# Seven block products in place of eight in the gate stage of a two-group decoder layer on eight cores

## The chip, the cores and the metric

One Trainium2 chip, all 8 cores. The metric is the device time of the slowest core, in microseconds. Two programs share the chip. Even cores ("half 0") take the first 976 positions of a prompt and a quarter of the sampling group, 1216 output columns each. Odd cores ("half 1") take the rest of the prompt, 1088 output columns, and recompute part of the first half for its state. Some executions fall in a slow state, in which one die, sometimes both, gets a lower clock. Unless said otherwise only fast runs are compared.

## The reference

One layer: a gated mixer of two branches, then a squared-ReLU feed-forward. The change touches the merge of the branches:

```python
xa, ga, q, k, v, g, gate_a, gate_b = split_proj(h @ w_in)      # h: rmsnorm(x), D_MODEL = 2048
...                                                            # ya: RG-LRU branch, yb: retention branch
merged = jax.nn.sigmoid(gate_a) * (ya @ p_a) + jax.nn.sigmoid(gate_b) * (yb @ p_b)
return merged @ w_out, new_buf, h_last, S_last
```

## The kernel before

Operations are recorded in program order with the memory they touch. A list scheduler then places each where it can start earliest by its own estimates of durations; every engine executes that order strictly. So an estimate decides the order of instructions, and a buffer decides what may be placed where. The estimate for VectorE ("dve"):

```python
elif meth == "tensor_tensor" and all(isinstance(x, bass.AP) and x.dtype in TWO for k, x in kw.items() if k != "op"):
    dur = 150 + 0.53 * n          # two-input operation, everything 16 bits wide, n elements per partition
```

The gate stage, behind the eight retention heads. `wA` and `wB` are block m of the two gates (16 x 128 x 128 each), `wp` the two branch projections:

```python
nE = min(6, (rt.e - rt.p) // al(4 * OW))
tb = [M.f32(rt(4 * OW), OW) for _ in range(nE)]
r1 = Reg(R1, A_R[2])
tb += [M.f32(r1(4 * OW), OW) for _ in range(16)]             # 22 temporaries
...
for m in range(16):
    wA, wB = wfm(40 + m), wfm(56 + m)
    wp = wload(T["w_p"][m], 2, 8, 128)
    for a, b in cf.och:                                       # three chunks of 362 or 364 columns (odd cores)
        n = b - a
        ts_ = []
        gops = []
        for w in (wA, wB):                                    # 2 x 16 matmuls
            pt = PT()
            gops.append(group(pt, w, hT, a + lead, b + lead))
            t = tnew()
            P.v("dve", "tensor_tensor", out=t[:, 0:n], in0=pt(0, n), in1=rbc[:, a + lead:b + lead], op=ALU.mult)
            P.v("act", "activation", out=t[:, 0:n], in_=t[:, 0:n], func=AF.Sigmoid)
            ts_.append(t)
        for z, y in enumerate((yaT, ybT)):                    # 2 x 8 matmuls
            ...
        P.v("pool", "tensor_tensor", out=mT[:, m, a:b], in0=ts_[0][:, 0:n], in1=ts_[1][:, 0:n], op=ALU.add)
```

The feed-forward's up and down stages (not shown) already compute each 2x2 arrangement of blocks with seven products and sums of weights and activations, the Strassen-Winograd scheme, in passes of 272 columns on odd cores.

Of the kernel before, what the change touches and what calls it, by code (L numbers as in the profile page):

```python
# [12 lines left out]
ALU = mybir.AluOpType  # L13
# [130 lines left out]
class Prog:  # L144
# [86 lines left out]
    def v(self, eng, meth, after=(), **kw):  # L231
        reads, writes, pr, pw = [], [], [], []
        n_ap = 0
        psum = False
        for k, x in kw.items():
            if isinstance(x, PV):
                (pw if k in ("out", "accum_out") else pr).append(x.pt)
                psum = True
            elif isinstance(x, bass.AP):
                (writes if k in ("out", "accum_out") else reads).append(x)  # L240
                if k in ("scale", "bias") or k.startswith("scalar"):
                    n_ap += 1
        n = self._n(kw["out"])
        tabs = None
        if meth == "bn_stats":
            dur = 280
        elif meth == "bn_aggr":
            dur = 175
        elif eng == "act":
            dur = (170 if psum else 225) + 0.833 * n + 45 * n_ap  # L250
            if meth == "activation":
                tabs = TABS.get(kw["func"])
        elif eng == "dve":
            if meth == "tensor_tensor_scan":
                dur = 90 + 2.5 * n
            elif meth == "reciprocal":
                dur = 60 + 6.5 * n
            elif meth in ("tensor_scalar", "tensor_copy", "tensor_scalar_mul") and not psum:
                dur = 190 + 0.66 * n
            elif meth == "tensor_tensor" and all(isinstance(x, bass.AP) and x.dtype in TWO for k, x in kw.items() if k != "op"):  # L260
                dur = 150 + 0.53 * n
            else:
                dur = (160 if psum else 220) + 1.05 * n + (100 if psum and n_ap > 1 else 0)
        elif meth == "tensor_tensor":
            dur = 260 + 1.92 * n
        elif meth == "tensor_copy":
            dur = 250 + 1.12 * n
        else:
            dur = 260 + 2.4 * n
        banks = self.banks  # L270

        def fn(e):
            a = {k: (x.ap(banks) if isinstance(x, PV) else x) for k, x in kw.items()}
            return getattr(e, meth)(**a)  # L274
        return self._new(eng, fn, reads, writes, pr, pw, dur, tabs, after=after)
# [375 lines left out]
    return v.rearrange("p (s t) -> p s t", t=3)  # L651

NSLOT = 7
HS = 16.0
US = 64.0
C0 = C_OFF["mask"][0]
# [9 lines left out]
A_VW = 0  # L666
# [4 lines left out]
def record(nc, P, M, T, cf):  # L671
# [19 lines left out]
            return a  # L691

    r3 = Reg(R3, A_CST)
    hT = M.bf(o_h, 16, NT)
    yaT = M.bf(o_ya, 8, NO)
    ybT = M.bf(o_yb, 8, NO)
    x1T = M.f32(0, 16, NO)
    Q = NO // 4
    RS, TS = 64 * Q, 48 * Q
# [6 lines left out]
    L_TMP = L_ACC + 4 * NO  # L706
    NTT = min(4, (A_KC - L_TMP) // (4 * Q))
    assert NTT >= 3
    mT = M.bf(A_R[2], 16, NO)
    assert A_R[2] + 32 * NO <= A_SLOT + 8192  # L710
    CW = max(b - a for a, b in cf.ch)
    OW = max(b - a for a, b in cf.och)
# [7 lines left out]
    def wload(src, *shape, at=None, after=()):  # L720
        if at is None:
            at = slots[wctr[0] % nring[0]]
            wctr[0] += 1
        w = M.bf(at, *shape)
        wf = w.rearrange("p a b -> p (a b)") if len(shape) == 2 else w.rearrange("p a b c -> p (a b c)")
        w_last[0] = P.dma("pool", wf, src, after=after)
        return w
# [253 lines left out]
    if cf.npre:  # L981
        NP = cf.npre
        NPT = len(cf.ptiles)
        hTq = M.bf(R2, 16, NP)
        rbcp = M.f32(R2 + 32 * NP, NP)
        assert R2 + 36 * NP <= R3
        r1 = Reg(R1, R2)
        Ls = [lru_set(r1, NP, 0, False) for _ in range(2)]
        vw, kw = M.bf(A_VW, 16, 512), M.bf(A_VW + 16384, 16, 512)
        nmax = 384  # L990
        vpp = M.bf(rt(1024 * NPT), NPT, 4, 128)
        kpp = [M.bf(rt(1024), 512) for _ in range(2)]
# [117 lines left out]
    o_cos = rt(4 * NT)  # L1110
    cosT = M.f32(o_cos, NT)
    sinT = M.f32(rt(4 * NT), NT)
    vq = [M.bf(r2(4096), 4, 512) for _ in range(2)] + [M.bf(o_yb + 4096 * i, 4, 512) for i in range(2)]
    assert o_yb + 8192 <= o_vh0

    def v_load(hg):
# [226 lines left out]
    for h in range(8):  # L1343
        if h < 7:
            proj(h + 1)
        attn(h)

    rt = Reg(TMPE, TEND)
    nE = min(6, (rt.e - rt.p) // al(4 * OW))
    tb = [M.f32(rt(4 * OW), OW) for _ in range(nE)]  # L1350
    r1 = Reg(R1, A_R[2])
    tb += [M.f32(r1(4 * OW), OW) for _ in range(16)]
    tc = [0]

    def tnew():
        x = tb[tc[0]]
        tc[0] += 1
        if tc[0] == len(tb):
            tc[0] = nE
        return x  # L1360

    del slots[0:2]
    nring[0] = len(slots)
    for m in range(16):
        wA, wB = wfm(40 + m), wfm(56 + m)
        wp = wload(T["w_p"][m], 2, 8, 128)
        for a, b in cf.och:
            n = b - a
            ts_ = []
            gops = []  # L1370
            for w in (wA, wB):
                pt = PT()
                gops.append(group(pt, w, hT, a + lead, b + lead))
# [1 line left out]
                P.v("dve", "tensor_tensor", out=t[:, 0:n], in0=pt(0, n), in1=rbc[:, a + lead:b + lead], op=ALU.mult)  # L1375
                P.v("act", "activation", out=t[:, 0:n], in_=t[:, 0:n], func=AF.Sigmoid)
                ts_.append(t)
            for z, y in enumerate((yaT, ybT)):
                pt = PT()
                P.mm([(pt(0, n), wp[:, z, k, :], y[:, k, a:b], k == 0, k == 7, "m") for k in range(8)], after=gops)  # L1380
                P.v("dve", "tensor_tensor", out=ts_[z][:, 0:n], in0=pt(0, n), in1=ts_[z][:, 0:n], op=ALU.mult)
            P.v("pool", "tensor_tensor", out=mT[:, m, a:b], in0=ts_[0][:, 0:n], in1=ts_[1][:, 0:n], op=ALU.add)


    accv = M.f32(L_ACC, NO)
# [9 lines left out]
    def sum_sq(m, x, a, b, e="pool"):  # L1395
        if m == 0:
            P.v("act", "activation", out=accv[:, a:b], in_=x, func=AF.Square)
        else:
            sq = sqs[m % 2]
            P.v("act", "activation", out=sq[:, 0:b - a], in_=x, func=AF.Square)  # L1400
            P.v(e, "tensor_tensor", out=accv[:, a:b], in0=accv[:, a:b], in1=sq[:, 0:b - a], op=ALU.add)

    def t_sums(src, t1, t2, t4, e=("dve",) * 4):

        b11, b12, b21, b22 = src
        P.v(e[0], "tensor_tensor", out=t1, in0=b12, in1=b11, op=ALU.subtract)
        P.v(e[1], "tensor_tensor", out=t2, in0=b22, in1=t1, op=ALU.subtract)
        P.v(e[2], "tensor_tensor", out=t4, in0=b21, in1=t2, op=ALU.subtract)
        P.v(e[3], "tensor_tensor", out=b12, in0=b22, in1=b12, op=ALU.subtract)

    spill = []
    wslots = [L_SLOT + 4096 * i for i in range(2, 6)]
# [1 line left out]
    for m in range(16):  # L1414
# [16 lines left out]
            spill.append(P.dma("sp", T["x1"][(m - 12) * 128 * NO:(m - 11) * 128 * NO].rearrange("(p n) -> p n", p=128), xt))  # L1431
        if m >= 8:
            i = m - 8
            t_sums([raw2[:, :, 4 * i + q, :] for q in range(4)], *[tq2[:, :, 8 * k + i, :] for k in range(3)])

    def rs_rows(a, b):
        pt = PT()
# [7 lines left out]
    def wset(src):  # L1445
# [4 lines left out]
        wb = M.hf(L_SLOT + 4096 * (2 * n % 6 + 1), 2, 1024)  # L1450
        for w, x in ((wa, src[0]), (wb, src[1])):
            P.dma("pool", w.rearrange("p a b -> p (a b)"), x)
        s1, s2, s4 = (M.hf(L_S + 2048 * ((3 * n + i) % 6), 1024) for i in range(3))
        a11, a12, a21, a22 = wa[:, 0, :], wa[:, 1, :], wb[:, 0, :], wb[:, 1, :]
        P.v("dve", "tensor_tensor", out=s1, in0=a21, in1=a22, op=ALU.add)
        P.v("dve", "tensor_tensor", out=s2, in0=s1, in1=a11, op=ALU.subtract)
        P.v("dve", "tensor_tensor", out=s4, in0=a12, in1=s2, op=ALU.subtract)
        P.v("dve", "tensor_tensor", out=a21, in0=a11, in1=a21, op=ALU.subtract)
        v = lambda x: x.rearrange("p (k c) -> p k c", k=8)
        return [v(x) for x in (a11, a12, s4, a22, s1, s2, a21)]  # L1460

    def prod(pt, w, x, first):
        P.mm([(pt(0, Q), w[:, k, :], x[:, k, :], first and k == 0, k == 7, "m" if first else "g") for k in range(8)])

    tmp = [M.f32(L_TMP + 4 * Q * i, Q) for i in range(NTT)]
    tmp_d = tmp + [M.f32(L_ACC + 4 * Q * i, Q) for i in range(4)]
# [94 lines left out]
    def u_sums(b, s, h):  # L1561
        j = 2 * b + 2 + s
        k = slice(4 * h, 4 * h + 4)
        r = rawq[j % 3][:, k]
        t = tq[j % 2][:, :, k]
        t_sums([r[:, :, q] for q in range(4)], *[t[:, i] for i in range(3)])

    def order(n, head):
        o = [(0, 0), (1, 0), (0, 1), (1, 1)] if head else [(0, 0), (0, 1), (1, 0), (1, 1)]
# [348 lines left out]
```

## Time and profile before

| | before |
|---|---|
| median of all 15 runs, this comparison | 2045.35 us |
| span, odd cores / even cores | 2036 to 2039 / 2024 to 2028 us |
| PE busy, slowest core | 95% |
| gate stage, odd cores | about 328 us |

The lines of the profile that carry this stand in the prediction. How to read them: PE is TensorE, DVE is VectorE, ACT is ScalarE and POOL is GpSimd; a bank is a piece of PSUM, the memory into which PE writes, and an evacuation is another engine's operation that reads a bank. "Busy" of a matmul is modelled, so durations come from periods; a bracket `[0.50 <-ACT arena L274]` says that the engine stood idle for 0.50 us until ACT finished; nearly all operations have the line of a recording helper (L274, L305, L307), so shapes tell them apart.

### The profile page before, as it was taken

How to read it: one execution, taken by the hardware profiler on the slowest of the kernel's cores; microseconds unless marked ns; L12 is line 12 of the kernel's file. 1: busy time of each engine (PE TensorE's matmuls, PEld its weight loads, DVE VectorE, ACT ScalarE, POOL GpSimd, SP SyncE). 2: the span in 40 equal slices, each digit the busy share in tenths (PEclk: the TensorE clock that was granted, in tenths of full speed). 3: DMA queues.
4: the chain of work that ended last, by engine and by line, in shares of the span. 5: the costliest groups of instructions: out<-in, count | busy, mean ns of one | idle time of the engine just before them, and what ended most of it. 6: DMA issues, size and time to landing. Idle time of an engine off the chain costs nothing.

```text
span 2039.2 us, 40316 instructions; the slowest of 8 cores (2024.5 to 2039.2 us)
## 1 busy us (share of the span) xinstructions
PE 1935.6 (95%) x14400; PEld 1384.5 (68%) x14400; DVE 1032.3 (51%) x1898; ACT 734.8 (36%) x1573; POOL 932.1 (46%) x1212
## 2 busy tenths in 40 slices
PE   4788799998999999999999999999999999999997
PEld 2444455555666666666678888888888778888567
DVE  3577634663334332222234565555556667675245
ACT  4455525675554411111123454444444111111123
POOL 5654752335666421211124454444444556555544
PEclk9998999999999999999999999999999999999998
DMA  8844732332332343443437766666667756565822
GB/s 224 145 104 117 160 74 42 54 61 43 66 65 45 55 83 63 82 74 63 73 84 147 177 126 157 135 123 126 127 126 163 175 108 137 86 159 85 187 78 99
DMA packets 83214, 219.20 MB, mean 107 GB/s; under 512 B 10176, under 2 KB 34496, under 8 KB 81216
## 3 DMA queue, kind: packets, MB, share of 16 engines
q0 software_dynamic: 38448, 139.05, 40.7%
q1 hardware_dynamic: 40816, 73.04, 11.0%
q10 hardware_dynamic: 3744, 4.46, 0.6%
q8 instruction: 118, 1.93, 0.4%
q14 instruction: 88, 0.72, 0.1%
HBM read 326.04 MB, written 29.51 MB: 174 GB/s over the span
## 4 chain that ended last, share of the span: by engine, by line
PE 83%; DVE 5%; issue 4%; DMA 4%; POOL 2%; ACT 2%; POOLq 0%; DVEq 0%; ACTq 0%; SPq 0%
PE bank L305 68%; PE bank L307 15%; DVE arena L274 5%; POOL arena L274 2%; DMA arena<-xo 2%; DMA arena<-w_tm 1%; ACT arena L274 1%; PE bank L303 0%; DMA arena<-w_dn 0%; POOL arena L321 0%; ACT L274 0%; DVEq L601 0%; POOLq L1726 0%; POOLq L601 0%; ACTq L601 0%
## 5 line engine op out<-in xcount | busy, mean ns | idle before, releaser
L305 PE MATMUL bank<-arena 128*128 128x272 f16 (+14 forms) x11408 | 1631.9, 302 | 69.9 <-DVE arena L274 50.0
L305 PEld LDWEIGHTS bank<-arena 128*128 128x128 bf16 (+3 forms) x11408 | 1098.8, 99 | 554.7 <-issue 97.5
L274 POOL TENSOR_TENSOR arena<-arena 128x272 f32<-128x272 f32 (+17 forms) x830 | 720.7, 880 | 651.8 <-DVE arena L274 402.5
L274 ACT ACTIVATE arena<-arena 128x272 f32<-128x272 f32 (+15 forms) x940 | 464.4, 518 | 797.8 <-DVE arena L274 608.3
L274 DVE TENSOR_TENSOR arena<-bank,arena 128x272 f32<-128x272 f32 (+8 forms) x794 | 391.0, 496 | 677.9 <-PE bank L305 478.9
L307 PE MATMUL bank<-arena 128*128 128x272 f16 (+3 forms) x2848 | 372.5, 278 | 21.1 <-POOL arena L274 9.5
L307 PEld LDWEIGHTS bank<-arena 128*128 128x128 f16 (+3 forms) x2848 | 277.6, 99 | 82.8 <-issue 28.8
L274 DVE TENSOR_TENSOR arena<-arena 128x1024 f16<-128x1024 f16 (+7 forms) x335 | 274.9, 832 | 33.3 <-ACT arena L274 13.1
L274 DVE SCALAR_TENSOR_TENSOR arena<-bank,arena 128x272 f32<-128x272 f32 (+6 forms) x392 | 170.8, 446 | 190.5 <-PE bank L305 118.2
L274 ACT ACTIVATE arena<-bank 128x272 f32<-128x272 f32 (+8 forms) x128 | 47.3, 374 | 304.9 <-PE bank L307 165.2
L274 DVE SCALAR_TENSOR_TENSOR arena<-arena 128x976 f32<-128x976 f32 (+5 forms) x110 | 125.3, 1169 | 33.3 <-ACT arena L274 32.4
L274 ACT COPY arena<-bank 64x384 f32<-64x384 f32 (+5 forms) x216 | 89.8, 424 | 78.6 <-DVE arena L274 30.9
L321 POOL DMA_DIRECT2D arena<-w_fm x80 | 45.5, 570 | 152.7 <-PE bank L305 133.8
L274 ACT ACTIVATE arena<-bank,arena 128x128 bf16<-128x128 f32 (+2 forms) x168 | 72.6, 513 | 34.4 <-PE bank L305 18.1
L321 POOL DMA_DIRECT2D arena<-w_up x64 | 37.6, 588 | 97.9 <-PE bank L307 87.6
L274 DVE TENSOR_SCALAR arena<-arena 128x384 bf16<-128x384 f32 (+5 forms) x104 | 57.0, 576 | 44.0 <-DMA arena<-xo 26.4
L274 ACT ACT_TABLE_LOAD x49 | 62.9, 1283 | 37.5 <-DVE arena L274 19.1
L321 POOL DMA_DIRECT2D arena<-w_dn x64 | 36.1, 566 | 61.7 <-DVE arena L274 37.9
L274 DVE TENSOR_TENSOR_SCAN arena<-arena 128x976 f32<-128x976 f32 (+1 forms) x16 | 38.5, 2406 | 6.4 <-POOL arena L274 6.4
L274 POOL COPY arena<-arena 128x3 f32<-128x3 f32 (+1 forms) x40 | 16.5, 413 | 53.1 <-DVE arena L274 46.2
L274 ACT CAST arena<-bank 128x128 bf16<-128x128 f32 x72 | 19.1, 266 | 42.6 <-PE bank L307 42.0
L274 POOL TENSOR_SCALAR arena<-arena 128x256 bf16<-128x256 f32 (+6 forms) x36 | 27.8, 788 | 12.1 <-DMA arena<-xp 7.2
(17 smaller groups left out, 110.2 us busy)
## 6 DMA issues: line engine op xcount, KB each, us to landing
arena<-w_fm POOLq DMA_DIRECT2D x80, 512.0 KB, 6.4
arena<-w_up POOLq DMA_DIRECT2D x64, 512.0 KB, 6.1
arena<-w_dn POOLq DMA_DIRECT2D x64, 512.0 KB, 6.9
u_hold<-arena SPq DMA_DIRECT2D x48, 272.0 KB, 3.7
arena<-u_hold SPq DMA_DIRECT2D x12, 1088.0 KB, 8.9
arena<-w_tm POOLq DMA_DIRECT2D x24, 512.0 KB, 10.4
arena<-xr SPq DMA_DIRECT2D x64, 136.0 KB, 3.6
arena<-w_o POOLq DMA_DIRECT2D x16, 512.0 KB, 6.4
```

Source lines behind the costliest of these rows:

```text
L274: return getattr(e, meth)(**a)
L305: r = e.matmul(out.ap(banks), lhsT=lhsT, rhs=rhs, start=start, stop=stop)
L307: r = e.matmul(out.ap(banks), lhsT=lhsT, rhs=rhs, start=start, stop=stop, skip_group_check=True)
L321: return e.dma_start(out=out, in_=in_)
```

## The change

Intent: gate blocks m = 2 to 15 with seven products instead of eight. The two gate blocks are the row halves of a 2x2 matrix, the two halves of the contraction its columns, and the tokens are split in two. Blocks 0 and 1 stay plain, to keep PE busy while VectorE forms the activation sums. Activations and weights become 16-bit floats with the longer fraction (`hf`), because sums of them are rounded too. The scheduler's estimate for 16-bit two-input operations rises. The core of the diff, cut where marked:

```diff
-                dur = 150 + 0.53 * n
+                dur = 291 + 0.529 * n
...
+GSTD = 2
...
-    hT = M.bf(o_h, 16, NT)
-    yaT = M.bf(o_ya, 8, NO)
-    ybT = M.bf(o_yb, 8, NO)
+    hT = M.hf(o_h, 16, NT)
+    yaT = M.hf(o_ya, 8, NO)
+    ybT = M.hf(o_yb, 8, NO)
...                                    (mT, the weight slots and the projections' weights likewise)
-    tb += [M.f32(r1(4 * OW), OW) for _ in range(16)]
...
+    tb = [M.f32(rt(4 * OW), OW) for _ in range(min(6, (rt.e - rt.p) // al(4 * OW)))]
...
-    for m in range(16):
-        wA, wB = wfm(40 + m), wfm(56 + m)
-        wp = wload(T["w_p"][m], 2, 8, 128)
+    for m in range(GSTD):
+        wA, wB, wp = gate_loads(m)
...                                    (the plain loop, as before)
+    H2 = NO // 2
+    hq = [hT[:, 8 * k:8 * k + 8, lead + H2 * n:lead + H2 * n + H2] for k in range(2) for n in range(2)]
+    TB = al(16 * H2)
+    th = [M.hf(a, 8, H2) for a in (R2, R2 + TB, R1 + TB, R1)]
+    for k in range(8):
+        t_sums([x[:, k, :] for x in hq], *[t[:, k, :] for t in th])
...
+    for m in range(GSTD, 16):
+        wA, wB, wp = gate_loads(m)
+        w = w_sums(*[x.rearrange("p (h k) c -> p h (k c)", h=2) for x in (wA, wB)], *[sring[(3 * m + i) % 6] for i in range(3)])
+        for s in range(2):
...
+            prod(X, a11, b11, True)
+            P.v("act", "copy", out=u2, in_=X(0, Q))
+            prod(Y, s2, t2, True)
+            P.v("dve", "tensor_tensor", out=u2, in0=Y(0, Q), in1=u2, op=ALU.add)
+            prod(Z, s1, t1, True)
+            P.v("dve", "tensor_tensor", out=y4, in0=Z(0, Q), in1=u2, op=ALU.add)
+            prod(W, s3, t3, True)
+            P.v("dve", "tensor_tensor", out=y4, in0=W(0, Q), in1=y4, op=ALU.add)
+            gate_out(y4, r2)
+            prod(X, a12, b21, False)
+            P.v("dve", "tensor_tensor", out=y1, in0=X(0, Q), in1=r1, op=ALU.mult)
+            gate_out(y1, None)
+            prod(Z, s4, b22, False)
+            P.v("dve", "tensor_tensor", out=y2, in0=Z(0, Q), in1=u2, op=ALU.add)
+            gate_out(y2, r2)
+            e = prod(W, a22, t4, False)
+            P.v("dve", "tensor_tensor", out=u2, in0=W(0, Q), in1=u2, op=ALU.add)
+            gate_out(u2, r1)
...                                    (four branch projections of 8 matmuls, the merge on pool)
```

More of the change, by code (lines that the diff above doesn't have):

```diff
@@ L708, in record @@
     assert NTT >= 3
-    mT = M.bf(A_R[2], 16, NO)
+    mT = M.hf(A_R[2], 16, NO)
     assert A_R[2] + 32 * NO <= A_SLOT + 8192
@@ L723, in wload @@
             wctr[0] += 1
-        w = M.bf(at, *shape)
+        w = M.hf(at, *shape)
         wf = w.rearrange("p a b -> p (a b)") if len(shape) == 2 else w.rearrange("p a b c -> p (a b c)")
@@ L983, in record @@
         NPT = len(cf.ptiles)
-        hTq = M.bf(R2, 16, NP)
+        hTq = M.hf(R2, 16, NP)
         rbcp = M.f32(R2 + 32 * NP, NP)
@@ L988, in record @@
         Ls = [lru_set(r1, NP, 0, False) for _ in range(2)]
-        vw, kw = M.bf(A_VW, 16, 512), M.bf(A_VW + 16384, 16, 512)
+        vw, kw = M.hf(A_VW, 16, 512), M.hf(A_VW + 16384, 16, 512)
         nmax = 384
@@ L1112, in record @@
     sinT = M.f32(rt(4 * NT), NT)
-    vq = [M.bf(r2(4096), 4, 512) for _ in range(2)] + [M.bf(o_yb + 4096 * i, 4, 512) for i in range(2)]
+    vq = [M.hf(r2(4096), 4, 512) for _ in range(2)] + [M.hf(o_yb + 4096 * i, 4, 512) for i in range(2)]
     assert o_yb + 8192 <= o_vh0
@@ L1346, in record, with t_sums, w_sums, prod @@
         attn(h)
+    def t_sums(src, t1, t2, t3, t4):
+        b11, b12, b21, b22 = src
+        P.v("dve", "tensor_tensor", out=t1, in0=b12, in1=b11, op=ALU.subtract)
+        P.v("dve", "tensor_tensor", out=t2, in0=b22, in1=t1, op=ALU.subtract)
+        P.v("dve", "tensor_tensor", out=t4, in0=b21, in1=t2, op=ALU.subtract)
+        P.v("dve", "tensor_tensor", out=t3, in0=b22, in1=b12, op=ALU.subtract)
+    def w_sums(wa, wb, s1, s2, s4):
+        a11, a12, a21, a22 = wa[:, 0, :], wa[:, 1, :], wb[:, 0, :], wb[:, 1, :]
+        P.v("dve", "tensor_tensor", out=s1, in0=a21, in1=a22, op=ALU.add)
+        P.v("dve", "tensor_tensor", out=s2, in0=s1, in1=a11, op=ALU.subtract)
+        P.v("dve", "tensor_tensor", out=s4, in0=a12, in1=s2, op=ALU.subtract)
+        P.v("dve", "tensor_tensor", out=a21, in0=a11, in1=a21, op=ALU.subtract)
+        v = lambda x: x.rearrange("p (k c) -> p k c", k=8)
+        return [v(x) for x in (a11, a12, s4, a22, s1, s2, a21)]
+    def prod(pt, w, x, first):
+        return P.mm([(pt(0, Q), w[:, k, :], x[:, k, :], first and k == 0, k == 7, "m" if first else "g") for k in range(8)])
+    del slots[0:2]
+    nring[0] = len(slots)
     rt = Reg(TMPE, TEND)
-    nE = min(6, (rt.e - rt.p) // al(4 * OW))
-    tb = [M.f32(rt(4 * OW), OW) for _ in range(nE)]
-    r1 = Reg(R1, A_R[2])
-    tb += [M.f32(r1(4 * OW), OW) for _ in range(16)]
+    tb = [M.f32(rt(4 * OW), OW) for _ in range(min(6, (rt.e - rt.p) // al(4 * OW)))]
     tc = [0]
     def tnew():
-        x = tb[tc[0]]
         tc[0] += 1
-        if tc[0] == len(tb):
-            tc[0] = nE
-        return x
-    del slots[0:2]
-    nring[0] = len(slots)
-    for m in range(16):
-        wA, wB = wfm(40 + m), wfm(56 + m)
-        wp = wload(T["w_p"][m], 2, 8, 128)
+        return tb[tc[0] % len(tb)]
+    def gate_loads(m):
+        return wfm(40 + m), wfm(56 + m), wload(T["w_p"][m], 2, 8, 128)
+    def p_group(wp, z, a, b, after):
+        pt = PT()
+        y = (yaT, ybT)[z]
+        P.mm([(pt(0, b - a), wp[:, z, k, :], y[:, k, a:b], k == 0, k == 7, "m") for k in range(8)], after=after)
+        return pt(0, b - a)
+    for m in range(GSTD):
+        wA, wB, wp = gate_loads(m)
         for a, b in cf.och:
             n = b - a
-            ts_ = []
-            gops = []
+            ts_, gops = [], []
             for w in (wA, wB):
@@ L1377, in record @@
                 ts_.append(t)
-            for z, y in enumerate((yaT, ybT)):
-                pt = PT()
-                P.mm([(pt(0, n), wp[:, z, k, :], y[:, k, a:b], k == 0, k == 7, "m") for k in range(8)], after=gops)
-                P.v("dve", "tensor_tensor", out=ts_[z][:, 0:n], in0=pt(0, n), in1=ts_[z][:, 0:n], op=ALU.mult)
+            for z in range(2):
+                P.v("dve", "tensor_tensor", out=ts_[z][:, 0:n], in0=p_group(wp, z, a, b, gops), in1=ts_[z][:, 0:n], op=ALU.mult)
             P.v("pool", "tensor_tensor", out=mT[:, m, a:b], in0=ts_[0][:, 0:n], in1=ts_[1][:, 0:n], op=ALU.add)
+    H2 = NO // 2
@@ new lines, in record @@
+    hq = [hT[:, 8 * k:8 * k + 8, lead + H2 * n:lead + H2 * n + H2] for k in range(2) for n in range(2)]
[3 more added lines that the diff above has]
+        t_sums([x[:, k, :] for x in hq], *[t[:, k, :] for t in th])
+    ra_, rb_ = Reg(R1 + 2 * TB, R2), Reg(R2 + 2 * TB, A_R[2])
+    sring = [M.hf(ra_(2048), 1024) for _ in range(6)]
+    tb = [M.f32(r(4 * Q), Q) for r in (rb_, ra_) for _ in range((r.e - r.p) // al(4 * Q))]
+    tc[0] = -1
@@ new lines, in gate_out @@
+    def gate_out(t, r):
+        if r is not None:
+            P.v("pool", "tensor_tensor", out=t, in0=t, in1=r, op=ALU.mult)
+        P.v("act", "activation", out=t, in_=t, func=AF.Sigmoid)
+    for m in range(GSTD, 16):
+        wA, wB, wp = gate_loads(m)
+        w = w_sums(*[x.rearrange("p (h k) c -> p h (k c)", h=2) for x in (wA, wB)], *[sring[(3 * m + i) % 6] for i in range(3)])
+        for s in range(2):
+            n1, n2 = Q * s, H2 + Q * s
+            b11, b21, b22 = (hT[:, 8 * k:8 * k + 8, lead + n:lead + n + Q] for k, n in ((0, n1), (1, n1), (1, n2)))
+            t1, t2, t3, t4 = (t[:, :, n1:n1 + Q] for t in th)
+            r1, r2 = rbc[:, lead + n1:lead + n1 + Q], rbc[:, lead + n2:lead + n2 + Q]
+            X, Y, Z, W = PT(), PT(), PT(), PT()
+            u2, y4, y1, y2 = (tnew() for _ in range(4))
+            a11, a12, s4, a22, s1, s2, s3 = w
+            prod(X, a11, b11, True)
[16 more added lines that the diff above has]
+            gate_out(u2, r1)
+            for t, z, n in ((y1, 0, n1), (y4, 1, n2), (y2, 0, n2), (u2, 1, n1)):
+                P.v("dve", "tensor_tensor", out=t, in0=p_group(wp, z, n, n + Q, [e]), in1=t, op=ALU.mult)
+            P.v("pool", "tensor_tensor", out=mT[:, m, n1:n1 + Q], in0=y1, in1=u2, op=ALU.add)
+            P.v("pool", "tensor_tensor", out=mT[:, m, n2:n2 + Q], in0=y2, in1=y4, op=ALU.add)
@@ L1401, in sum_sq @@
             P.v(e, "tensor_tensor", out=accv[:, a:b], in0=accv[:, a:b], in1=sq[:, 0:b - a], op=ALU.add)
-    def t_sums(src, t1, t2, t4, e=("dve",) * 4):
-        b11, b12, b21, b22 = src
-        P.v(e[0], "tensor_tensor", out=t1, in0=b12, in1=b11, op=ALU.subtract)
-        P.v(e[1], "tensor_tensor", out=t2, in0=b22, in1=t1, op=ALU.subtract)
-        P.v(e[2], "tensor_tensor", out=t4, in0=b21, in1=t2, op=ALU.subtract)
-        P.v(e[3], "tensor_tensor", out=b12, in0=b22, in1=b12, op=ALU.subtract)
     spill = []
@@ L1433, in record @@
             i = m - 8
-            t_sums([raw2[:, :, 4 * i + q, :] for q in range(4)], *[tq2[:, :, 8 * k + i, :] for k in range(3)])
+            v = [raw2[:, :, 4 * i + q, :] for q in range(4)]
+            t1, t2, t4 = (tq2[:, :, 8 * k + i, :] for k in range(3))
+            t_sums(v, t1, t2, v[1], t4)
     def rs_rows(a, b):
@@ L1452, in wset @@
             P.dma("pool", w.rearrange("p a b -> p (a b)"), x)
-        s1, s2, s4 = (M.hf(L_S + 2048 * ((3 * n + i) % 6), 1024) for i in range(3))
-        a11, a12, a21, a22 = wa[:, 0, :], wa[:, 1, :], wb[:, 0, :], wb[:, 1, :]
-        P.v("dve", "tensor_tensor", out=s1, in0=a21, in1=a22, op=ALU.add)
-        P.v("dve", "tensor_tensor", out=s2, in0=s1, in1=a11, op=ALU.subtract)
-        P.v("dve", "tensor_tensor", out=s4, in0=a12, in1=s2, op=ALU.subtract)
-        P.v("dve", "tensor_tensor", out=a21, in0=a11, in1=a21, op=ALU.subtract)
-        v = lambda x: x.rearrange("p (k c) -> p k c", k=8)
-        return [v(x) for x in (a11, a12, s4, a22, s1, s2, a21)]
-    def prod(pt, w, x, first):
-        P.mm([(pt(0, Q), w[:, k, :], x[:, k, :], first and k == 0, k == 7, "m" if first else "g") for k in range(8)])
+        return w_sums(wa, wb, *[M.hf(L_S + 2048 * ((3 * n + i) % 6), 1024) for i in range(3)])
     tmp = [M.f32(L_TMP + 4 * Q * i, Q) for i in range(NTT)]
@@ L1565, in u_sums @@
         t = tq[j % 2][:, :, k]
-        t_sums([r[:, :, q] for q in range(4)], *[t[:, i] for i in range(3)])
+        v = [r[:, :, q] for q in range(4)]
+        t_sums(v, t[:, 0], t[:, 1], v[1], t[:, 2])
     def order(n, head):
```

## The prediction

> **What bounds the kernel now.** I read the cores first, then the engine line of the page, then busy times by stage, then PE's waits, and last the timeline where two stages meet. Unless said otherwise a reading is of core 7, the slowest.
>
> ```profile
> core 6: 2027.6 us, clock 0.990
> core 7: 2039.2 us, clock 0.987
> ```
>
> Odd cores (1088 own columns, 2036 to 2039 us) set the end; even cores (1216 own columns) finish some 12 us earlier. All clocks are near full, so this is the fast state, and the change has to be counted for the odd cores.
>
> ```profile
> PE 1935.6 (95%) x14400; PEld 1384.5 (68%) x14400; DVE 1032.3 (51%) x1898; ACT 734.8 (36%) x1573; POOL 932.1 (46%) x1212
> ```
>
> PE is the candidate, but a mean over stages can hide another bound. The table of stretches gives start:end, length, busy us (and instructions) of PE, PEld, DVE, ACT and POOL, granted clock, DMA share, GB/s:
>
> ```profile
> 780.00:840.00 60.00, 60.00 (x393) 38.18 (x391) 17.38 (x33) 8.10 (x16) 11.44 (x15) 1.00 0.37 64
> 1300.00:1400.00 100.00, 100.00 (x866) 84.46 (x865) 57.36 (x124) 45.79 (x123) 45.08 (x61) 1.00 0.63 127
> ```
>
> The first is the gate stage (about 717 to 1041 us), the second the up-projection, which already uses seven products in place of eight. PE is full in both at clock 1.00 and nothing else is near full. So PE columns removed from the gate stage come off the end one for one, unless something new stops PE.
>
> Busy time of a matmul is modelled, so for its cost I take periods. Two evacuations of the same place in neighbouring token chunks of the gate stage:
>
> ```profile
> 1021.71 0.54 DVE L274 TENSOR_TENSOR arena<-bank,arena 128x362 f32<-128x362 f32 x1 [1.92 <-PE bank L305]
> ...
> 1029.07 0.53 DVE L274 TENSOR_TENSOR arena<-bank,arena 128x362 f32<-128x362 f32 x1 [1.92 <-PE bank L305]
> ```
>
> A chunk is 48 matmuls: 7.36 us / 48 = 153.3 ns at 362 columns. At 272 columns the chain that ended last gives start, duration, what and count:
>
> ```profile
> 1231.62 2.78 PE bank L307 x24
> ...
> 1244.59 2.78 PE bank L307 x24
> ```
>
> These are the same point of two neighbouring passes, two column halves apart, 112 matmuls: 12.97 us / 112 = 115.8 ns.
>
> **What the Trainium skill says.** "TensorE: Matmul & The Clock Gate", section "Wait — 56ns, not 53.3ns?": start to start is columns / 2.4 GHz plus about 2.5 ns. That gives 153.3 and 115.8 ns: the trace agrees, so more but shorter matmuls pay a small fixed fee each. The peak-current note in "Seeing it yourself" speaks of 13/16 of the clock once three cores of a die run dense matmuls; the profiled run shows 0.987 to 0.993 on all eight, so I do not use it. "VectorE: DVE Perf Modes", section "The perf-mode tier table", says a two-input 16-bit operation reaches two elements per cycle, and "SBUF — State Buffer", section "SBUF: two separate sides", says that VectorE with two SBUF inputs and GpSimd take one port pair by turns, the loser waiting for the whole instruction. The trace agrees with both; the same operation twice, free and behind three POOL instructions:
>
> ```profile
> 1660.02 0.68 DVE L274 TENSOR_TENSOR arena<-arena 128x1024 f16<-128x1024 f16 x1
> ...
> 1661.53 2.19 POOL L274 TENSOR_TENSOR arena<-arena 128x272 f32<-128x272 f32 x3
> 1661.78 2.50 DVE L274 TENSOR_TENSOR arena<-arena 128x1024 f16<-128x1024 f16 x1
> ```
>
> **The change part by part.** (1) *Fewer products.* Blocks m = 2 to 15 of the gates now treat two gate blocks by two halves of the contraction by two halves of the tokens as a 2x2 product with seven block products. Columns of the gates per m: before 2 x 16 x 1088 = 34816, after 7 x 8 x 1088/2 = 30464. The branch projections keep 16 x 1088. In instructions: before 144 matmuls x 153.3 ns (7.36 x 3 chunks, 22.1 us), after 2 x 7 x 8 + 4 x 16 = 176 x 115.8 ns = 20.4 us. Saved per m: 4352/2.4 ns less 32 x 2.5 ns = 1.73 us; times 14: 24.3 us. On even cores, 4864 columns per m, 27.3 us; they stay the faster ones.
>
> (2) *Sums of activations*, once: 32 operations of 128x544 in 16 bits, at 0.44 us free and 580 ns in the mean of today's rows: 14 to 19 us of VectorE. They need neither PE nor a bank. In the order of the changed program's instructions all 32 stand ahead of the second product that needs them: eight before the attention stage, most between its last evacuations. PE has 168 further matmuls of 362 or 364 columns (25.8 us) behind the attention's last transposes. So: hidden, 0 us.
>
> (3) *Sums of weights*, per m: 4 operations of 128x1024, 712 ns each in the up stage (841 over all): 3 us. VectorE's evacuations go from 12 x 0.54 = 6.4 us to 20 x 0.44 = 8.8 us. Total some 12 of 20.4 us. POOL, per m: 10 x 0.82 us plus three DMA issues of 0.57 = 9.9 us; ACT 10 x 0.42 = 4.2 us. All below PE, at about the shares of the up stage (57, 45, 46 of 100), where PE never stops. But VectorE must not be late: behind W's first product PE has just one product (0.93 us) before it accumulates into that bank again, and an evacuation of 0.44 us with two handovers fits only if VectorE is free. A weight sum held by POOL as above would break it now and then. I take 2 us in all for 28 passes, an estimate.
>
> (4) *Weights*: the same three loads per m, cast to another 16-bit type. Landing takes 6.4 us; gate loads of the next m find their slots free one m ahead. 0 us. The rows of 128x272 f16 and 128x272 bf16 both read 279 ns, so the type costs PE nothing.
>
> (5) *Fewer spare buffers at the seam.* Today the first gate blocks fill PE's holes at the end of the attention:
>
> ```profile
> 708.41 7.89 PE L305 MATMUL bank<-arena 64*64 64x128 bf16 x50
> 716.13 0.52 PE L303 MATMUL bank<-arena 128*128 128x128 bf16 x5
> 716.58 43.65 PE L305 MATMUL bank<-arena 128*128 128x362 bf16 x283
> ```
>
> The merged row of 50 is 2 of the attention and 48 of the gates, over the normalisation's latency. The gate temporaries were 22 and can now be only six until m = 2; each chunk holds two until the last head is done. In the order of instructions, 192 gate matmuls stood before those transposes; now there are 120 and one product of eight. Missing: 72 x 153.3 - 8 x 115.8 = 10.1 us of filling. Not all of it is lost, as many fillers were longer than the hole (16 matmuls, 2.5 us, where an unfilled handover to ACT reads 0.50 us). In the last hole 4.6 us of work (24 x 153.3 + 8 x 115.8) now stand over about 7.4 us: 2.8 us idle. Add one or two unfilled handovers: 3 us lost.
>
> (6) *The scheduler's estimate* for 16-bit sums rises (for 1024 elements from 693 to 833 ns), which reorders the feed-forward too. PE waits 8.3 us for VectorE there in 13 waits; I expect between 3 us won and 3 us lost, 0 in the middle.
>
> Sum: -24.3 + 2 + 3 + 0 = -19.3 us, from a median of 2045.75: about 2026 us, 1.0% less.
>
> **The rivals.** *A, VectorE or the port lock becomes the bound in the gates.* For it: the 2.50 us row, and two more POOL additions per pass than the up stage has. Against it: the up stage with the same sums has no PE wait, and a gate pass is 88 matmuls (10.2 us) against 56. If each pass lost 0.7 us, 20 us would go and the time would stay at 2045. *B, the seam costs the whole 10 us*, or the sums placed between the attention's evacuations delay its serial state updates: 2033 us. For it, PE follows ACT there one step at a time; against it, the lost filler is partly overlong. *C, nothing is lost and the better estimate helps:* -24.3 - 3, 2018 us. *D, 16-bit floats with a longer fraction draw more current and a lower clock:* some per cent slower; against it, the feed-forward runs f16 at clock 1.00. *E, the even cores become the slowest:* no, they gain more.
>
> **Range and chances.** C and B bound the likely cases, with room at both ends: 2018 to 2034. Faster by over 2% would need under 2005, 41 us, more than all columns removed: 1%. Slower by over 2% would need D or a stall of 65 us: 1%. Within 2%: 98%.
>
> **What would show it.** Step 1: in the gate stage, from one block to the next, 20.4 us in place of 22.1, with 14 x 144 = 2016 fewer matmuls of 362 and 364 columns and 14 x 176 = 2464 more of 272. Step 3: PE's waits for VectorE in the gate stage, some 2 us; 10 or more means A. Step 5: PE idle of 3 us between the last head's projections and the last transposes; near 10 means B. Step 6: PE's waits in the feed-forward, 8.3 us today. Step 2: no PE wait for VectorE at the first products of m = 2. I am wrong in kind if PE is no longer full in the gates, or if the clocks fall.

## The result, and the profile after

The changed kernel took 2020.35 us (median of 7 runs) beside 2045.35 us of the kernel before (15 runs). The ratio of the fast runs is 0.9879, with a 95% interval of 0.9867 to 0.9891: 1.2% less, inside the 2%. A ratio here is the mean time of one kernel's fast runs over that of the other's in the same rounds, so not quite the ratio of the medians. The outputs are correct.

Spans and clocks of the changed kernel, core 7 again, and core 1, which was slowest this time:

```profile
core 1: 2020.5 us, clock 0.982
...
core 7: 2015.7 us, clock 0.985
```

The gate stage, the same table of stretches as in the prediction, core 7:

```profile
740.00:1020.00 280.00, 279.81 (x2416) 234.35 (x2414) 152.27 (x328) 56.46 (x135) 125.02 (x175) 1.00 0.44 75
```

PE is still full (279.8 of 280 us), at clock 1.00; VectorE went from 29 to 54 of 100, ACT stays low and POOL is at 45. One block of the new gates, on PE's timeline of core 7: the same place in two neighbouring blocks.

```profile
883.23 1.09 PE L307 MATMUL bank<-arena 128*128 128x272 f16 x8
...
903.61 1.09 PE L307 MATMUL bank<-arena 128*128 128x272 f16 x8
```

That is 20.38 us a block.

So where did 23 to 25 us come from? I cut the run at eight instructions that exist in both kernels: VectorE's last scan of the RG-LRU, the first and the twelfth normalised retention output (the multiplication of 128x512 from PSUM), PE's last transposes of the attention, the first scaled residual of the output projection, the first and last store of the up stage, the last load of the down stage, and the end. All are start times from the timelines, so each stretch holds waits and work together. Core 7, with differences taken before rounding (the other odd cores agree to some 1.6 us in each stretch behind the first):

| stretch, us | before | after | difference |
|---|---|---|---|
| start to last scan | 475.3 | 477.6 | +2.3 |
| to first retention output ("attention start") | 38.6 | 41.8 | +3.1 |
| to twelfth ("heads") | 151.0 | 150.3 | -0.7 |
| to last transposes ("seam") | 51.2 | 43.3 | -7.8 |
| to output projection ("gate") | 327.6 | 313.9 | -13.8 |
| output projection | 140.9 | 140.8 | -0.1 |
| up stage | 400.2 | 400.6 | +0.4 |
| down stage | 301.6 | 294.3 | -7.3 |
| last load to end | 152.8 | 153.2 | +0.5 |

Seam and gate belong together, for 10.1 us of gate matmuls only moved from in front of the last transposes to behind them. The two ends of the gate stretch, first before, then after: PE's last transposes and the first scaled residual.

```profile
716.13 0.52 PE L303 MATMUL bank<-arena 128*128 128x128 bf16 x5
1043.78 0.36 DVE L274 TENSOR_SCALAR arena<-arena 128x272 f16<-128x272 f32 x1
```

```profile
712.97 0.52 PE L303 MATMUL bank<-arena 128*128 128x128 bf16 x5
1026.82 0.36 DVE L274 TENSOR_SCALAR arena<-arena 128x272 f16<-128x272 f32 x1
```

Heads, seam and gate make 529.8 us before and 507.5 after on core 7: -22.3 (odd cores in the mean: 529.7 and 507.8). The first row has the same instruction order in both kernels on every engine. It varies from core to core, from 474 to 475 us before and from 476 to 481 us after, and the granted clock of this stretch goes with it: core 1 had 0.96 and 475.3 us before, 0.95 and 481.1 us after; over all the runs below, odd cores at 0.97 took 474 to 476 us and one at 0.93 took 484.8 us. So I don't count it as an effect of the change. That leaves three things to settle: +3.1 at the attention's start (+3.2 in the mean of the odd cores), -7.3 in the down stage, and how the -22.3 divides.

*The attention's start.* VectorE, core 7, before: scan, then evacuations of the first head's projections:

```profile
479.41 0.56 DVE L274 TENSOR_TENSOR arena<-bank,arena 128x384 f32<-128x384 f32 x1 [0.51 <-POOL arena L274]
484.60 0.56 DVE L274 TENSOR_TENSOR arena<-bank,arena 128x384 f32<-128x384 f32 x1 [4.63 <-POOL arena L274]
```

and after:

```profile
481.67 0.56 DVE L274 TENSOR_TENSOR arena<-bank,arena 128x384 f32<-128x384 f32 x1 [0.52 <-POOL arena L274]
482.14 7.64 DVE L274 TENSOR_TENSOR arena<-arena 128x544 f16<-128x544 f16 x8
489.70 0.94 DVE L274 TENSOR_TENSOR arena<-bank,arena 128x384 f32<-128x384 f32 x2
```

The scheduler put eight activation sums into a hole of 4.63 us. Free, they would take 8 x 0.44 = 3.5 us; they took 7.64 us, while POOL was working on five wide operations (below). The single records fit the lock that the prediction names: the first five sums took 1.98 and four times 1.23 us, one to each POOL operation, and the last three, with POOL done, 0.43 us each.

```profile
481.58 6.84 POOL L274 TENSOR_TENSOR arena<-arena 128x1088 f16<-128x1088 f32 x5
```

The next evacuation follows its predecessor by 8.0 us in place of 5.2. PE pays behind it: 0.8 us more in a wait for POOL (3.5 against 2.7 us), and 2.1 us more at the first state update; before, then after:

```profile
486.97 0.26 PE L307 MATMUL bank<-arena 128*128 128x128 bf16 x1 [1.06 <-ACT arena L274]
```

```profile
492.06 0.26 PE L307 MATMUL bank<-arena 128*128 128x128 bf16 x1 [3.11 <-ACT arena L274]
```

*The down stage.* PE's waits from 1160 to 1900 us (waiting engine, engine waited for, us, times, longest), before and then after:

```profile
PE bank L307 <- DVE arena L274: 6.1, 8, 1.9
PE bank L305 <- DVE arena L274: 2.2, 5, 0.8
PE bank L305 <- POOL arena L274: 1.0, 1, 1.0
```

```profile
PE bank L307 <- DVE arena L274: 1.3, 2, 1.0
PE bank L307 <- ACT arena L274: 0.2, 1, 0.2
```

7.0 us less waiting for VectorE, and the down stage is 7.3 us shorter. The change doesn't touch this stage except through the estimate and a helper's argument order.

*The seam.* The last hole of the attention, after (core 7):

```profile
707.99 5.14 PE L305 MATMUL bank<-arena 64*64 64x128 bf16 x34
712.97 0.52 PE L303 MATMUL bank<-arena 128*128 128x128 bf16 x5
713.42 2.79 PE L305 MATMUL bank<-arena 128*128 128x272 f16 x19
```

There is no wait in it, although 2.8 us of idle time had been forecast there: the last transposes come 5 us after the group of matmuls in front of the hole, where they had come 7.7 us after it with more filler. The filler had stretched the hole, not only filled it. The runs below agree: with 34, 42 and 50 matmuls in this row, of which two belong to the attention, the transposes come 5.0, 6.5 and 7.7 us after its start, without a wait (42 in runs 4, 7 and 12).

### The profile page after: what moved, and what is told of

Same layout as the page of the kernel before. It is cut to its first block, busy times and chain, and to the rows that moved or that the text cites. A ratio compares the mean times of both kernels' runs of the same rounds, so it can differ in the third digit from the quotient of the medians.

```text
span 2020.5 us, 41951 instructions; the slowest of 8 cores (1993.4 to 2020.5 us)
## 1 busy us (share of the span) xinstructions
PE 1918.5 (95%) x14848; PEld 1429.3 (71%) x14848; DVE 1127.8 (56%) x2098; ACT 753.7 (37%) x1629; POOL 1000.9 (50%) x1310
## 4 chain that ended last, share of the span: by engine, by line
PE 86%; DMA 4%; issue 3%; DVE 3%; POOL 2%; ACT 1%; SPq 0%; POOLq 0%; DVEq 0%; ACTq 0%
PE bank L305 65%; PE bank L307 20%; DVE arena L274 3%; POOL arena L274 2%; DMA arena<-xo 2%; DMA arena<-w_tm 1%; ACT arena L274 1%; DMA arena<-rtp 1%; DMA arena<-w_up 1%; PE bank L303 0%; POOL arena L321 0%; SPq L321 0%; ACT L274 0%; POOLq L1783 0%; DVEq L601 0%
## 5 line engine op out<-in xcount | busy, mean ns | idle before, releaser
L305 PE MATMUL bank<-arena 128*128 128x272 f16 (+11 forms) x11184 | 1548.2, 296 | 69.4 <-DVE arena L274 54.3
L305 PEld LDWEIGHTS bank<-arena 128*128 128x128 f16 (+2 forms) x11184 | 1079.7, 99 | 477.8 <-issue 102.3
L274 POOL TENSOR_TENSOR arena<-arena 128x272 f32<-128x272 f32 (+15 forms) x928 | 787.9, 859 | 621.1 <-DVE arena L274 366.0
L274 ACT ACTIVATE arena<-arena 128x272 f32<-128x272 f32 (+14 forms) x968 | 472.5, 509 | 743.5 <-DVE arena L274 464.5
L274 DVE TENSOR_TENSOR arena<-bank,arena 128x272 f32<-128x272 f32 (+7 forms) x906 | 423.4, 471 | 576.0 <-PE bank L305 361.7
L307 PE MATMUL bank<-arena 128*128 128x272 f16 (+1 forms) x3520 | 461.6, 278 | 19.7 <-POOL arena L274 9.6
L307 PEld LDWEIGHTS bank<-arena 128*128 128x128 f16 (+1 forms) x3520 | 341.4, 99 | 95.9 <-issue 27.9
L274 DVE TENSOR_TENSOR arena<-arena 128x1024 f16<-128x1024 f16 (+7 forms) x423 | 347.9, 833 | 30.8 <-ACT arena L274 17.2
L274 ACT COPY arena<-bank 128x272 f32<-128x272 f32 (+5 forms) x244 | 100.7, 420 | 101.1 <-PE bank L305 42.3
L274 DVE TENSOR_SCALAR arena<-arena 128x384 f16<-128x384 f32 (+5 forms) x104 | 56.4, 570 | 45.2 <-DMA arena<-xo 26.9
L274 POOL COPY arena<-arena 128x3 f32<-128x3 f32 (+1 forms) x40 | 16.2, 404 | 49.5 <-DVE arena L274 44.1
```

What stands on the lines that cost most here:

```text
L274: return getattr(e, meth)(**a)
L305: r = e.matmul(out.ap(banks), lhsT=lhsT, rhs=rhs, start=start, stop=stop)
L307: r = e.matmul(out.ap(banks), lhsT=lhsT, rhs=rhs, start=start, stop=stop, skip_group_check=True)
```

## The experiments

The theory after the result: (1) fewer products give 24.3 us; (2) eight sums at the attention's start cost 3.2; (3) the seam costs some 2; (4) the scheduler's estimate gives some 7 in the feed-forward. Rivals: the feed-forward gains through some other effect of the change, or the products give less and the rest more; the 3.2 us are chance. There were twelve runs, of nine variants and the changed kernel itself, all correct, each with 5 rounds against the kernel before. Stretches are means over the odd cores unless a core is named.

**1. The estimate alone**, in the kernel before.

```diff
-                dur = 150 + 0.53 * n
+                dur = 291 + 0.529 * n
```

> The kernel before with nothing changed but the scheduler's estimate for 16-bit two-input sums (0.291 us + 0.529 ns per element in place of 0.150 us + 0.53 ns). Theory 1 (the feed-forward gained some 7 us from the better estimate alone, as the stretch from the last store of the up stage to the last load of the down stage shrank from 301.5 to 294.3 us on core 7): the same stretch reads 294 to 295 us, the waits of PE for VectorE in the feed-forward fall from 8.3 us to under 2 us, and the time falls by 6 to 8 us (ratio 0.9965). Rival (the gain comes from the gate stage handing over differently, or from the chip of that run): the stretch stays at 301 us and the ratio is 1.000.

Ratio 0.9961 (0.9947 to 0.9975). The down stage reads 293.4 to 294.0 us; the stretches from the attention's start to the up stage stay within 1 us of those before. PE's waits from 1160 to 1900 us, core 7:

```profile
PE bank L307 <- DVE arena L274: 1.3, 2, 1.1
PE bank L305 <- POOL arena L274: 1.1, 1, 1.1
PE bank L305 <- DMA arena<-u_hold: 0.7, 1, 0.7
PE bank L307 <- ACT arena L274: 0.2, 1, 0.2
```

The rival falls: one line of the estimate, with no work removed, gives about 8 us of time (5 to 11 by the interval) and 7.5 us of the down stage; with the up stage and the last stretch, which got longer, 5.9 us remain in the stretches. The same operation of 1024 elements had means of 712 ns in the up stage (1200 to 1540 us) and 1013 ns in the down stage (1600 to 1880 us) of the kernel before, against 693 ns in the old estimate and 833 ns in the new. In this run the down stage's mean is no shorter (1114 ns); what changed is the order around these operations. Which places in the order matter was not traced, and only this one other estimate was tried, so that a truer estimate is what helps, and not just another order, isn't shown.

**2. The changed kernel with the old estimate.**

```diff
-                dur = 291 + 0.529 * n
+                dur = 150 + 0.53 * n
```

> The changed kernel with the old estimate. Theory 1: it gives back 6 to 8 us of the 25, the stretch of the down stage reads 301 us, ratio to before about 0.9915, and the gate stage from the attention's last transposes to the output projection stays within 1 us of 313.9 us. Rival: ratio stays at 0.988.

Ratio 0.9909 (0.9895 to 0.9923). Up and down stage together take 698.7 to 701.0 us, against 694.8 to 695.4 after the change and 700.3 to 702.1 before. Core 7's waits for VectorE are back at 7.6 us in 15 waits. The effect is there from both sides, about 5 us of stretches this time; part of it moved into the up stage (402 to 404 us), so "the down stage reads 301" was wrong in place (it reads 294 to 299). Seam and gate together stay within 2 us of the changed kernel.

**3. The third activation sum later.** Its eight operations may only start after the sixth head.

```diff
+        if h == 5:
+            hold = [P.ops[-1]]
...
-        t_sums([x[:, k, :] for x in hq], *[t[:, k, :] for t in th])
+        t_sums([x[:, k, :] for x in hq], *[t[:, k, :] for t in th], after=hold)
```

Inside `t_sums` only the operation that writes t3 takes `after`.

> The changed kernel with the third activation sum (eight operations) tied behind the sixth head of the attention, so that they no longer stand at the start of the attention stage. Theory 2 (those eight sums, 7.64 us of VectorE while POOL held the port, delayed the evacuation that the first transposes and state updates wait for, 3.1 us on core 7): from the last scan to the first normalised head the time falls back from 41.7 to 38.7 us (as before the change), and the kernel gains 3 us against the changed one (ratio 0.9865 against 0.988). Rival (the sums are hidden, and the 3 us are the later start of this run): no gain, the distance stays at 41.7 us, or the sums only press on a later head and the 3 us reappear there.

The attention's start is back at 38.7 to 39.2 us on all odd cores; heads, seam and gate together stay at 507.8 to 508.4. Ratio 0.9860 (0.9844 to 0.9875). VectorE on core 7, at the place where the sums had stood:

```profile
482.84 0.56 DVE L274 TENSOR_TENSOR arena<-bank,arena 128x384 f32<-128x384 f32 x1 [0.52 <-POOL arena L274]
488.02 0.56 DVE L274 TENSOR_TENSOR arena<-bank,arena 128x384 f32<-128x384 f32 x1 [4.63 <-POOL arena L274]
```

The hole of 4.63 us is back, to the hundredth. So the 3.2 us are the sums', not chance, and they don't reappear later. The stretches show it; the interval of the ratio overlaps that of the changed kernel.

**4. Twelve temporaries at the seam** on odd cores.

```diff
-    tb = [M.f32(rt(4 * OW), OW) for _ in range(min(6, (rt.e - rt.p) // al(4 * OW)))]
+    tb = [M.f32(rt(4 * OW), OW) for _ in range(min(12, (rt.e - rt.p) // al(4 * OW)))]
```

> The changed kernel with 12 gate temporaries in place of 6 on odd cores (even cores have room for 6 only), so 216 gate matmuls stand before the attention's last transposes in place of 120 and 8. Theory 3 (six temporaries leave PE 2 us idle at the seam): PE's waits between 690 and 720 us fall from about 2 us to about 0, and the kernel gains 2 us against the changed one (ratio 0.987). Rival A (the filler that was missing was overlong anyway): within 0.5 us of the changed kernel. Rival B: with only 72 matmuls (11 us) left behind the transposes, the activation sums come late and PE waits for VectorE at the first products: slower by 1 us or more.

Ratio 0.9865 (0.9851 to 0.9879). Heads, seam and gate take 506.9 us against 507.8 in the changed kernel: 1.0 us gained, half of what was expected and more than rival A allows; rival B falls, for nothing got slower. In the window that was named before the run, 690 to 720 us, PE's waits on core 7 are gone (0 against 1.2 us), but the seam now ends 14 us later; between 660 and 740 us they did not vanish: 3.2 us against 3.5. With more filler, heads and seam take 13 us longer and the gate stretch 14 us less. The time's ratio is lower than the stretches explain, but its interval overlaps that of the changed kernel.

**5. One plain block instead of two.**

```diff
-GSTD = 2
+GSTD = 1
```

> The changed kernel with one plain gate block at the seam in place of two (blocks 1 to 15 use seven products). One more block saves 1.73 us of PE. Theory (the plain blocks are there to give VectorE time for the activation sums): with 24 matmuls of 362 or 364 columns (3.7 us) left behind the attention's last transposes in place of 168, PE waits for VectorE at the first products, 3 us or more, so the kernel is 1 to 4 us slower than the changed one although its matmul work is less. Rival (the sums are done by then anyway): 1.7 us faster than the changed kernel, heads + seam + gate 506.1 us in place of 507.8.

The theory of this run was wrong. Heads, seam and gate take 506.2 to 507.2 us; the changed kernel in the same rounds (run 8) has 507.6 to 509.8. The sums are ready in time even with 24 plain matmuls left; PE waits 0.7 us for POOL and 0.4 us for a weight load between 690 and 760 us, and not at all for VectorE. Ratio 0.9891 (0.9866 to 0.9917), beside 0.9904 (0.9882 to 0.9926) for run 8: the right direction, not resolved by the times alone.

**6. The number type alone**, in the kernel before: `bf` to `hf` for hT, yaT, ybT, mT and the weights.

> The kernel before with hT, yaT, ybT, mT and the weights in the other 16-bit float type, nothing else. Prediction's step 4: no stage differs by over 0.5 us, clock as before, ratio 1.000 within its interval. Rival D (a longer fraction costs clock or PE time): ratio 1.005 or more, or lower clocks in fast runs.

Ratio 1.0017 (0.9990 to 1.0044). Heads, seam and gate read 529.7 to 530.4 us; before, 529.0 to 530.1. "No stage differs by over 0.5 us" did not hold: the up stage reads up to 407 us on this chip. But so does that of the other kernels of these rounds (408 us in run 7), and the granted clock of the stage was lower: 0.98 on the core with 407.1 us, 1.00 on core 7, which reads 401.9. No cost of the type is seen, though this interval leaves room for one of 9 us; run 12, which has the type too, narrows it. The down stage reads 297 to 301 us here with the old estimate, so its length alone is a loose measure. Up and down stage together, on cores that had the full clock throughout the up stage, make 698.7 to 702.1 us in every run with the old estimate and 694.4 to 695.9 in every run with the new one.

**7. Runs 3 and 4 together.**

> The changed kernel with both the third sum tied behind the sixth head and 12 temporaries on odd cores. If the two gains are independent: 3.2 us (attention start back to 38.7 us) and 0.9 us (heads + seam + gate 506.9 us as with 12 temporaries alone), so 4 us faster than the changed kernel. If they collide (the eight sums fall among the fillers and delay the evacuations or the first products): 3 us or less.

Attention start 37.0 to 39.2 us (mean 38.4, 3.8 less than in run 8), heads, seam and gate 505.7 to 507.2 us (mean 506.5, 1.9 less than run 8's 508.4). They do not collide. Ratio 0.9865 (0.9844 to 0.9885).

**8. The changed kernel again**, in the rounds of runs 5 to 7.

> The changed kernel itself, so that the others of this call are set against it in the same rounds: ratio 0.988 and the same stage lengths as in its first trace within 0.5 us each (attention start 42, heads 150.4, seam 43.5, gate 313.9, up and down together 695), with only the time up to the last scan varying from core to core and run to run.

Ratio 0.9904 (0.9882 to 0.9926), overlapping the first 0.9879. Attention start 41.9 to 42.6, heads 150.4, seam 42.9 to 44.1, gate 313.9 to 315.6. The up stage reads 400.7 to 404.9 us here; it had been 400.5 to 401.4. So "within 0.5 us each" fails there, and on core 5 in the gate: the clock of the up stage was 0.99 on the core with 404.9 us and 1.00 on the one with 400.7.

**9 and 11. The best of the above: third sum later, one plain block.** The edits of runs 3 and 5 together.

> The changed kernel with the third sum tied behind the sixth head and one plain block in place of two. If both gains seen alone add up: attention start 38.7 us (3.2 less than the changed kernel), heads + seam + gate 506.2 us (1.7 less), so 4.9 us faster than the changed kernel; ratio to before some 0.985 in rounds where the changed one has 0.988. If the later sums now come too late for the single plain block: PE waits for VectorE at the first products and the gain is 3 us or less.

All timed runs of this call were in the slow state of one die, so they give no ratio. On the undisturbed die, cores 5 and 7, heads, seam and gate read 507.2 and 506.2 us. It was run again:

> The same kernel as the run with the third sum later and one plain block, whose timed runs all fell in the slow state of one die. On an undisturbed chip: ratio to before 0.985 (0.0025 under the changed kernel's 0.988), and on all odd cores attention start 38.7 us and heads + seam + gate 506.2 us.

Median 2013.53 us (4 runs) beside 2042.50 (11 runs); ratio 0.9859 (0.9842 to 0.9876). Attention start 38.6 to 38.8 us, heads, seam and gate 506.1 to 506.8 us on all odd cores: the two gains add up in the stretches, 3.3 and 1.6 us against the changed kernel's means. Its ratio is the lowest, but only 0.0001 under that of run 3, and its interval overlaps that of the changed kernel and that of run 3.

**10 and 12. The main part taken out:** all 16 blocks plain, everything else of the change kept. The activation sums are computed and not used; the sums of weights go with the products.

```diff
     for m in range(GSTD, 16):
-        wA, wB, wp = gate_loads(m)
-        w = w_sums(...)
-        for s in range(2):
...
+        plain(m)
```

> The changed kernel with its main part taken out: all 16 gate blocks plain, everything else of the change kept (activation sums computed but unused, six temporaries at the seam, type, estimate). Step 1 (24.3 us from fewer columns): heads + seam + gate return to 531.6 us (2168 plain matmuls behind the transposes at 153.3 ns, 336 us in the gate column), 24 us more than the changed kernel's 507.8; attention start stays at 42 us; up and down stay at 695 us; so the time ends within 3 us of the kernel before, ratio about 0.9995. Rival (the products gain much less and the feed-forward much more): heads + seam + gate under 525 us, ratio 0.996 or less.

Again the slow state; on cores 5 and 7 the gate column reads 336.2 and 336.7 us. Run again:

> The same kernel as the run with all gate blocks plain, again because of the slow state. On an undisturbed chip: ratio to before 0.9995 within its interval (0.998 to 1.001), gate column some 336 us on all odd cores.

Ratio 1.0003 (0.9989 to 1.0018). On all odd cores the gate stretch takes 336.2 to 336.3 us, and heads, seam and gate together 531.4 to 532.0 (mean 531.8). The two ends of the gate stretch on core 7:

```profile
712.69 0.52 PE L303 MATMUL bank<-arena 128*128 128x128 bf16 x5
1048.93 0.36 DVE L274 TENSOR_SCALAR arena<-arena 128x272 f16<-128x272 f32 x1
```

This splits the difference: against the changed kernel's 507.8 the products, with all that they need of the other engines, give 24.0 us, and against 529.7 before, with the same matmuls, the seam costs 2.1 us. The rest of the change, +3.2 and +2.1 and -5.9 in the feed-forward (up, down and last stretch), makes some -0.6 us, inside the interval of the ratio.

## Why the prediction was right or wrong

The range held: 2020.35 lies in 2018 to 2034, and "within 2%" came true. The centre, 2026, was 6 us too high: the estimate gave more and the gate stage's evacuations cost less than forecast, the activation sums cost what was not forecast, and errors of both signs met in the sum. That the range held is in part luck: run 3, which takes the unforeseen 3.2 us back, has a median of 2017.14 us (2044.35 for the kernel before in the same rounds), below the range's lower end.

- **Step 1, fewer products, 24.3 us: right.** Run 12 against the changed kernel gives 24.0 us; the block period is 20.38 us where 20.4 was forecast.
- **Step 2, activation sums, 0 us: wrong.** The step counted VectorE's free time at the end of the attention and looked at the eight early sums only to say that they are early enough. It did not ask what stands behind them in VectorE's strict order. They cost 3.1 us on core 7 (3.2 in the mean), and runs 3, 7 and 11 take them back. The sign that the step named, no wait of PE for VectorE at the first products of m = 2, came true, but it looked at the other end of the attention. The prediction had the mechanism in rival B, and the port lock in a fence, but tied neither to this place.
- **Step 3, evacuations late in the gate stage, 2 us: too high.** From 740 to 1025 us PE waits for VectorE once, for 0.2 us, on core 7. Rival A falls.
- **Step 4, weights and type, 0 us: right** within what the times resolve (runs 6 and 12).
- **Step 5, the seam, 3 us: about right in size, wrong in place.** 2.1 us by run 12. The forecast hole at the last transposes has no wait; PE's waits between 660 and 740 us grew from 2.0 to 3.5 us, mostly at the handovers to ACT in the chain of state updates. Twelve temporaries give back 1.0 of the 2.1 us (run 4); the cause of the rest is open.
- **Step 6, the estimate, 0 in the middle, 3 us either way: mis-sized.** Run 1 shows 7.5 us in the down stage, 5.9 us with the up stage and the last stretch; run 2 shows about 5 from the other side. The step had the right row, 8.3 us of waits for VectorE in the feed-forward, and took their removal for as likely as their growth. Rival C, that the better estimate helps, was the nearest of the rivals in time (2018), for a reason half right: something was lost at the attention's start and the seam, and the estimate gave about twice what C allowed.
- **Rivals D and E** fall: clocks in the gate stage stayed at 1.00, and even cores stayed faster (1993 to 2002 us against 2013 to 2020).

The sum with measured terms for core 7: -24.0 (531.4 to 507.5) + 1.6 (529.8 to 531.4) + 3.1 - 6.4 (up, down and last stretch) - 0.1 (output projection) + 2.3 from the start is -23.5, and its span fell by 23.5. It closes by construction, since the stretches make up the span; only how the -22.3 of heads, seam and gate divides is an independent reading (run 12). What stays open: which reorderings in the down stage remove the waits, half of the seam's cost, and whether the clock alone moves the start.

## What to carry to other kernels

Where PE is full, removed columns can be priced from two periods, at columns / clock plus a small fee per matmul: here 24.3 us by this price and 24.0 measured. The misses were all in the auxiliary work. For each operation that a scheduler may place early, look at what stands behind it in its engine's order and who holds the same port at that moment, and give it an earliest point as well as a deadline. Where a scheduler runs on estimates, try fitting them to the mean durations of the profile, contention included: here that one line was worth about a quarter of the whole gain, though why the new order is better was not traced.

## What the Trainium skill lacked or had wrong

- "TensorE: Matmul & The Clock Gate", section "Back-to-back issue gap", says that in a stream of weight loads and matmuls the spacing at 512 columns is about 131 ns and that columns / 2.4 + 2.5 over-counts there. In this kernel, with one weight load per matmul, 362 columns took 153.3 ns and 272 columns 115.8 ns, just what the formula gives.
- "SBUF — State Buffer", section "SBUF: two separate sides", states the lock between VectorE with two SBUF inputs and GpSimd. The page gives two slowdowns, by which engine starts first, without the operations, and no size for streams of operations that meet. Here eight sums of 0.44 us took 7.64 us beside five POOL operations, by turns with them, while one 1024-element sum stood through three POOL operations in a row (2.50 us, in the prediction's lines), and the mean of one 1024-element sum, 0.68 us when free, ranged from 0.71 us (up stage) to 1.01 us (down stage) in the kernel before.
